# Modulation sums issued a step later, value products in batches of three, a ring of four and a fifth split-weight tile

## The chip, the core and the metric

One core of a Trainium2 chip runs the whole program. The metric is the device time of one execution in microseconds (us). Three executions of the kernel before took 1661.31, 1668.17 and 1668.65 us, with a median of 1668.17 us.

## What is computed

A trunk of two layers. Each layer normalises 512 latent and 256 context tokens of width 1024, shifts and scales them with rows that a small matrix-vector product makes of a conditioning vector (the "modulation"), projects them once, runs three kinds of attention (A: windowed, 8 heads; B: 2-D neighbourhood, 4 heads; C: latent, 4 heads), adds the output projection under a gate, and then a squared-ReLU MLP under a gate. In the last layer the context is only needed as keys and values.

```python
mod = split(silu(c) @ w_ada[l] + b_ada[l], 6)        # 6 rows of 1024, for latent and for context
h = modulate(rmsnorm(x, g1), mod[0], mod[1]) @ w_in[l]
x = x + mod[2] * (concat(out_a, out_b, out_c) @ w_out[l])
x = x + mod[5] * (relu(modulate(rmsnorm(x, g2), mod[3], mod[4]) @ w1) ** 2 @ w2)
```

## The kernel before

All data are float32. A projection with 32-bit precision is made of three matmuls on TensorE: weight and activation are each split into a rounded high part and a low part, and high·high, high·low and low·high are added up in PSUM. So every weight block that is loaded (`raw`, 128x1024) is first turned into two tiles: ScalarE casts the high part `wh` (L460) and VectorE subtracts to get the low part `wl` (L461). Both come from one set of tiles with the tag `w4`, four in all: two weight blocks at a time.

**Attention.** `att_unit` (L595) handles four rows of 128 queries. TensorE makes scores (L614), VectorE evacuates them with a running minimum (L618, L625), ScalarE takes the exponential (L630), VectorE, ScalarE or GpSimd normalises (L634 to L638). Then for every block of 128 keys, a "turn" transposes the four probability tiles on TensorE (L665) into PSUM (two tiles `pst`), and ScalarE or VectorE copies the 128x512 result to a slot of the ring `pT_ring` (L670), which has `NPT` = 6 slots. A "product" is the pair of value matmuls of one key block (L679). Turns and products go in batches of `PVB` = 6 key blocks: first all turns of a batch, from the last to the first, then all its products, so that the batch begins with a product that waits for the newest copy. A unit has 2, 4, 5 or 6 key blocks, so it is one batch. There are 40 units.

**Modulation.** The first rows come from matmuls at the start (`ada_quarter`, L249) and during layer 0 (`ada_row`, L207). The MLP gate of layer 0 and the six rows of layer 1 are made on the side during the MLP of layer 0 by the generator `ada_dve` (L269). A step of it loads a 128x512 piece of the weights (`araw`, L279), and VectorE multiplies it with a column of the conditioning vector and adds it to an accumulator `acc` (L283, L285); two accumulators for latent and context, or one where only the latent row is needed. Sixteen steps make a row. Then a matmul with a matrix of ones sums the accumulators over the partitions (L291, called the sum below), and a few small operations and transfers finish the row. `step(n)` in the MLP code (L1181) runs n steps after each weight chunk, 97 in all; what is left runs after the last MLP group of layer 0 (L1191). The sum of a row is issued in the same call that begins the next row. Accumulators, `araw` tiles and the ReLU results of the MLP share nine 128x512 tiles with the tag `re`.

**MLP.** `mlp1` computes 128 hidden features at a time over all tokens (24 or 48 matmuls for a weight block, L1099 to L1101), `mlp2` adds four such blocks to the output (L1133 to L1135), `resid` multiplies with the gate (L735) and adds to the stream (L736).

**Order.** A scheduler sets the order on each engine: it simulates the program with its own costs, takes what is ready by priority (products and sums have a high one) and gives out tiles of a tag as they come free. Each engine then runs its list strictly in order, so an instruction that waits holds everything behind it. `FENCE` (L76) makes a few weight loads of the start wait for the arrival of a given load of modulation weights.

Of the kernel before, what the change touches and what calls it, by code (L numbers as in the profile page):

```python
# [28 lines left out]
HUGE = 3e38  # L29
PS = {"d": 2, "s": 3, "t": 2, "v": 1, "a": 1}  # L30
STEPS = 2
PVB = 6
NPT = 6
ADAB = 2
STEP5 = 3
PREP1 = 1
# [3 lines left out]
XN = "VA"  # L40
RFAST = "GV"
PUT = "A"
CAPS = {"tm": 4, "rt": 4, "pr": 8, "r0": 16, "re": 9, "raw": 4, "w4": 4, "xn": 12,
        "h1": 16, "h2": 16, "pg": 18, "cr": 1, "ct": 8, "kr": 5, "vc": 2, "kc": 8,
        "up": 4, "u": 16, "wf": 16, "of": 8, "fg": 2, "ga": 4}
PAD = ("pr", "tm", "xn", "pg", "up")
# [2 lines left out]
for _tag, _names in (  # L49
    ("tm", "ce tf shuf qkraw maskB rpb junk upraw qr uphi"),  # L50
    ("rt", "rtmp brow ar"),
    ("pr", "prob"),
    ("r0", "raw0"),
    ("re", "relu acc araw arow"),
    ("raw", "raw"),
    ("w4", "wh wl"),
    ("xn", "xn"),
    ("h1", "hT1"),
    ("h2", "hT2"),
    ("pg", "qs kh kl vtok bias oth otl"),  # L60
    ("cr", "craw"),
    ("up", "uph upl"),
    ("ct", "cth ctl ropeC"),
    ("kr", "krf krh krl qrh qrl"),
    ("vc", "vc"),
    ("kc", "kc qc"),
    ("u", "uh ul of fg"),
    ("wf", "wfh wfl"),
    ("ga", "gate"),
):  # L70
    for _n in _names.split():
        TAGS[_n] = _tag
ADAPOS = [9, 18, 27]
FIN = ["vv", "vv", "gg", "gW"]
RLAST = "VV"
FENCE = {"pw0": 4, "pw1": 6, "w3": 24, "w4": 30, "rA": 31, "mA": 31}  # L76


@with_exitstack
def hybrid_dit_kernel(  # L80
# [30 lines left out]
    def prob(n, name="prob"):  # L111
        return sbuf(n, F32, name)

    def view(t_, shape):
        n = int(np.prod(shape))
        t_ = t_[:, :n]
        return t_ if len(shape) == 1 else t_.rearrange("p (a b) -> p a b", a=shape[0])
# [68 lines left out]
    V.tensor_scalar(nsink, sink, -1.0, None, ALU.mult)  # L186
    pT_ring = cp.tile([P, NPT, 512], F32, name="pT_ring")
    pT_n = [0]
# [80 lines left out]
    def ada_dve(l, ms):  # L269


        for m in ms:
            nw = 1 if l == DEPTH - 1 and m > 1 else 2
            acc = [[prob(512, name="acc") for _ in range(2)] for _ in range(nw)]
            for h in range(2):
                for k in range(KC):
                    raw = temp(512, name="araw")
                    c0 = m * D + h * 512
                    nc.sync.dma_start(raw, w_ada[l, k * P:(k + 1) * P, c0:c0 + 512])  # L279
                    for w in range(nw):  # L280
                        a_ = acc[w][h]
                        if k == 0:
                            V.tensor_scalar(a_, raw, ct[:, k, w:w + 1], None, ALU.mult)  # L283
                        else:
                            V.scalar_tensor_tensor(a_, raw, ct[:, k, w:w + 1], a_, ALU.mult, ALU.add)  # L285
                    yield

            ps = ps_d()
            with tc.high_priority():
                for j in reversed(range(2 * nw)):  # L290
                    T.matmul(ps[32 * j:32 * j + 32, :], ones, acc[j // 2][j % 2], start=True, stop=True,  # L291
                             tile_position=(0, 32 * j))
            rows = slice(0, 64 * nw)
            if m in (2, 5):
                gd = dp.tile([2, D], F32, name=f"gate{l}_{m}")
                br = prob(512, name="arow")
                for j in range(2 * nw):
                    c0 = m * D + (j % 2) * 512
                    nc.sync.dma_start(br[32 * j:32 * j + 32], b_ada[l:l + 1, c0:c0 + 512].partition_broadcast(32))
                V.tensor_tensor(br[rows], br[rows], ps[rows], ALU.add)  # L300
                for j in range(2 * nw):
                    nc.sync.dma_start(gd[j // 2:j // 2 + 1, (j % 2) * 512:(j % 2 + 1) * 512],
                                      br[32 * j:32 * j + 1])
                gdram[l, m] = gd
            else:
                mt = cp.tile([P, KC, 2], F32, name=f"mod{l}_{m}")
                ar = prob(512, name="arow")
                V.tensor_copy(ar[rows], ps[rows])
                pt = ps_d()
                for q in range(4):  # L310
                    T.transpose(pt[:, q * P:q * P + 64 * nw], ar[rows, q * P:(q + 1) * P], ident[rows, rows])
                p4 = pt.rearrange("p (q j c) -> p q j c", q=4, j=4)
                for w in range(nw):
                    V.tensor_tensor(mt[:, :, w].rearrange("p (h q) -> p q h", h=2), p4[:, :, 2 * w:2 * w + 2, 0],
                                    bT[:, l, m, :].rearrange("p (h q) -> p q h", h=2), ALU.add)
                modT[l, m] = mt
            ada_done.add((l, m))
# [277 lines left out]
    def att_unit(kind, rows, vap, put, sinkcols=None):  # L595
# [88 lines left out]

        for i in range(0, len(order), PVB):
            for item in reversed([turn(kb, i + j) for j, kb in reversed(list(enumerate(order[i:i + PVB])))]):
                product(*item)
# [51 lines left out]
    for l in range(DEPTH):  # L739
# [126 lines left out]
        if l == 0:  # L866
            rA = const([2, 512], ropeA, "ropeA")
# [446 lines left out]
```

## Time and profile before

| | |
|---|---|
| median of three executions | 1668.17 us (1661.31 to 1668.65) |
| the profiled execution | 1664.65 us |
| its span from first to last instruction | 1662.8 us |
| TensorE busy | 1596.6 us (96%) |
| TensorE weight loads busy (beside the matmuls) | 1364.9 us (82%) |
| VectorE busy | 1031.8 us (62%) |
| ScalarE busy | 689.4 us (41%) |
| GpSimd busy | 614.3 us (37%) |
| mean granted TensorE clock | 0.988 of full |

Instructions are named by their line of the kernel before (L291). An arrow `psd<-acc,ones` gives the output tile and the inputs; PE is TensorE, DVE VectorE, ACT ScalarE, POOL GpSimd, SP the queue that issues the transfers. The granted clock is a share of 2.4 GHz: 0.50 is 1.2 GHz. "Idle before" is the time an engine stood still ahead of an instruction, with what ended it.

### The profile page before, as it was taken

The numbers are of one execution on the slowest core, as the hardware profiler recorded it, in microseconds if no ns is written. First come the engines' busy times: TensorE is split into PE (matmuls) and PEld (weight loads), VectorE is DVE, ScalarE is ACT, GpSimd is POOL, SyncE is SP. The second block draws the span as 40 slices with busy tenths as digits, with TensorE's granted clock in tenths as the row PEclk, the third lists the DMA queues.
The fourth block names the chain that finished last, engine by engine and source line by source line (L and its number), as shares of the span: only waits on it lengthen the run. The fifth ranks groups of instructions, "written<-read, shape, count | busy, mean of one in ns | idle before, by whom it ended". The sixth has DMA issues, their size and how long they took to land.

```text
span 1662.8 us, 24084 instructions
## 1 busy us (share of the span) xinstructions
PE 1596.6 (96%) x8994; PEld 1364.9 (82%) x8994; DVE 1031.8 (62%) x1995; ACT 689.4 (41%) x1342; POOL 614.3 (37%) x564
## 2 busy tenths in 40 slices
PE   6999999999999999999999999999999899999997
PEld 3888789777898998988989789878776788888886
DVE  3565866787887576554455966776786644444446
ACT  5454467655631222312213154536765532332332
POOL 1111743643424253341523431143462333333335
PEclk8999999999999999999999999999999999999999
DMA  9653401120243333334333613211130133333331
GB/s 314 183 164 114 143 27 47 59 65 1 81 154 126 125 103 111 114 103 129 95 104 119 226 39 91 58 47 51 44 90 25 45 101 98 92 102 93 97 120 58
DMA packets 156421, 164.46 MB, mean 99 GB/s; under 512 B 8960, under 2 KB 111368, under 8 KB 156304
## 3 DMA queue, kind: packets, MB, share of 16 engines
q1 hardware_dynamic: 156304, 162.92, 32.2%
q8 instruction: 71, 1.16, 0.3%
q14 instruction: 46, 0.38, 0.1%
HBM read 155.53 MB, written 2.12 MB: 95 GB/s over the span
## 4 chain that ended last, share of the span: by engine, by line
PE 84%; DVE 7%; ACT 3%; DMA 2%; issue 2%; POOL 1%; SPq 1%; POOLq 0%; DVEq 0%; ACTq 0%
PE psd L1100 8%; PE psd L1099 8%; PE psd L1101 8%; PE psv L679 5%; PE pss L614 5%; PE pst L665 4%; PE pss L1133 3%; PE pss L1134 3%; PE pss L1135 3%; PE psd L477 3%; PE psd L479 3%; PE psd L478 3%; DVE wl L461 2%; PE psv L1133 1%; PE psa L1134 1%
## 5 line engine op out<-in xcount | busy, mean ns | idle before, releaser
L460 ACT CAST wh<-raw 128x1024 fp32r<-128x1024 f32 (+1 forms) x168 | 175.3, 1044 | 514.5 <-PE psd L1100 186.2
L461 DVE TENSOR_TENSOR wl<-raw,wh 128x1024 fp32r<-128x1024 f32 (+1 forms) x168 | 221.5, 1319 | 253.1 <-ACT wh L460 252.4
L736 POOL TENSOR_TENSOR xlat<-xlat,rtmp 128x512 f32<-128x512 f32 x159 | 236.9, 1516 | 263.6 <-DVE rtmp L735 261.9
L1099 PE MATMUL psd<-hT,wh 128*128 128x384 f32 (+2 forms) x752 | 265.8, 354 | 4.5 <-DVE hT L424 3.0
L1100 PE MATMUL psd<-hT,wl 128*128 128x384 f32 (+2 forms) x752 | 264.9, 352 | 3.7 <-DVE wl L461 3.7
L1101 PE MATMUL psd<-hT,wh 128*128 128x384 f32 (+2 forms) x752 | 265.3, 353 | 0.3 <-POOL hT L426 0.3
L638 POOL TENSOR_TENSOR prob<-prob,sm 128x512 f32<-128x512 f32 (+3 forms) x110 | 126.8, 1160 | 273.0 <-DVE sm L631 205.1
L1108 POOL TENSOR_TENSOR relu<-relu 128x384 f32<-128x384 f32 (+1 forms) x96 | 93.5, 976 | 332.5 <-ACT uh L1107 284.6
L630 ACT ACTIVATE prob<-prob,m 128x513 f32<-128x513 f32 (+6 forms) x160 | 120.9, 756 | 102.0 <-DVE m L625 58.7
L1099 PEld LDWEIGHTS psd<-hT,wh 128*128 128x128 f32 x752 | 141.7, 189 | 18.4 <-DVE hT L424 3.5
L1100 PEld LDWEIGHTS psd<-hT,wl 128*128 128x128 f32 x752 | 141.9, 189 | 14.3 <-DVE wl L461 4.6
L1101 PEld LDWEIGHTS psd<-hT,wh 128*128 128x128 f32 x752 | 141.7, 188 | 10.1 <-POOL hT L426 0.9
L285 DVE SCALAR_TENSOR_TENSOR acc<-araw,consts,acc 128x512 f32<-128x512 f32 x140 | 132.2, 968 | 6.3 <-DMA araw<-in_w_ada_dram 5.4
L1109 DVE TENSOR_TENSOR ul<-relu,uh 128x384 fp32r<-128x384 f32 (+1 forms) x96 | 60.7, 633 | 92.4 <-POOL relu L1108 92.3
L665 PE MATMUL pst<-consts,prob 128*128 128x128 f32 x688 | 106.6, 278 | 4.3 <-POOL prob L638 3.2
L665 PEld LDWEIGHTS pst<-consts,prob 128*128 128x128 f32 x688 | 80.6, 141 | 27.3 <-issue 11.2
L477 PE MATMUL psd<-hT,wh 128*128 128x384 f32 (+1 forms) x280 | 97.8, 349 | 2.3 <-ACT wh L460 1.3
L479 PE MATMUL psd<-hT,wl 128*128 128x384 f32 (+1 forms) x280 | 96.9, 347 | 1.1 <-DVE wl L461 1.1
L478 PE MATMUL psd<-hT,wh 128*128 128x384 f32 (+1 forms) x280 | 96.8, 346 | 0.0
L1134 PE MATMUL pss<-wl,uh 128*128 128x512 f32 x224 | 87.5, 390 | 0.0
L1135 PE MATMUL pss<-wh,ul 128*128 128x512 f32 x224 | 87.2, 390 | 0.0
L1106 ACT ACTIVATE relu<-psd 128x384 f32<-128x384 f32 (+1 forms) x93 | 48.6, 522 | 92.8 <-PE psd L1101 92.8
(265 smaller groups left out, 3550.8 us busy)
## 6 DMA issues: line engine op xcount, KB each, us to landing
raw<-in_w_mlp_in_dram SPq DMA_DIRECT2D x64, 512.0 KB, 4.3
raw<-in_w_mlp_out_dram SPq DMA_DIRECT2D x64, 512.0 KB, 4.4
araw<-in_w_ada_dram SPq DMA_DIRECT2D x112, 256.0 KB, 4.7
raw<-in_w_in_dram SPq DMA_DIRECT2D x24, 512.0 KB, 5.5
raw<-in_w_ada_dram SPq DMA_DIRECT2D x24, 512.0 KB, 4.3
raw<-in_w_ada_dram SPq DMA_DIRECT2D x32, 256.0 KB, 6.0
raw<-in_w_out_dram SPq DMA_DIRECT2D x8, 512.0 KB, 4.4
raw<-in_w_out_dram SPq DMA_DIRECT2D x16, 256.0 KB, 3.5
```

The source lines that it names most:

```text
L460: A.copy(hi, raw)
L461: V.tensor_tensor(lo, raw, bc(hi), ALU.subtract)
L477: T.matmul(ps[:, :n], wh[:, k, :], hh[k][:, s0:s0 + n], start=(k == 0), stop=False)
L478: T.matmul(ps[:, :n], wh[:, k, :], hl[k][:, s0:s0 + n], start=False, stop=False)
L479: T.matmul(ps[:, :n], wl[:, k, :], hh[k][:, s0:s0 + n], start=False, stop=(k == KC - 1))
L665: T.transpose(pt[:, r * P:(r + 1) * P], pts[r][:, pos[r][kb]:pos[r][kb] + P], ident)
L736: (V if fast and (RLAST if fast == "end" and t == 3 else RFAST)[dh] == "V" else G).tensor_tensor(xt[t][:, cs], xt[t][:, cs], tmp, ALU.add)
L1099: T.matmul(o_, wh[:, k, :], hh[k][:, sl], start=(k == 0), stop=False)
L1100: T.matmul(o_, wl[:, k, :], hh[k][:, sl], start=False, stop=False)
L1101: T.matmul(o_, wh[:, k, :], hl[k][:, sl], start=False, stop=(k == KC - 1))
L1134: T.matmul(a_, uh[:, ts_], wl[:, c % 2, :], start=False, stop=False)
L1135: T.matmul(a_, ul[:, ts_], wh[:, c % 2, :], start=False, stop=fin)
```

## The change

- `PVB` 6 to 3 and `NPT` 6 to 4: turns and products now go three key blocks at a time, and the ring has four slots. A unit of 4 to 6 key blocks becomes two batches.
- The four accumulators of a row become one 128x2048 tile with a tag of its own, `ac`, of which there is one. The tag `re` falls from nine tiles to five.
- `ada_dve` yields once more ahead of the sum. A row takes 17 steps in place of 16, and its sum comes a step after its last accumulation.
- The tag `w4` rises from four tiles to five. The memory in use stays the same: the ring gives up 4 KB per partition and `w4` takes them; `re` gives up 8 KB and `ac` takes them.
- The fence of the weight load of columns 1152 on waits for load 5 of the modulation weights in place of load 30.

```diff
-PVB = 6
-NPT = 6
+PVB = 3
+NPT = 4
-CAPS = {"tm": 4, "rt": 4, "pr": 8, "r0": 16, "re": 9, "raw": 4, "w4": 4, "xn": 12,
+CAPS = {"tm": 4, "rt": 4, "pr": 8, "r0": 16, "re": 5, "ac": 1, "raw": 4, "w4": 5, "xn": 12,
-    ("re", "relu acc araw arow"),
+    ("re", "relu araw arow"),
+    ("ac", "acc"),
-FENCE = {"pw0": 4, "pw1": 6, "w3": 24, "w4": 30, "rA": 31, "mA": 31}
+FENCE = {"pw0": 4, "pw1": 6, "w3": 24, "w4": 5, "rA": 31, "mA": 31}
@@ ada_dve
-            acc = [[prob(512, name="acc") for _ in range(2)] for _ in range(nw)]
+            acc = view(prob(2048, name="acc"), [4, 512])
+            acc = [[acc[:, 2 * w + h_] for h_ in range(2)] for w in range(nw)]
             for h in range(2):
                 for k in range(KC):
...
                     yield
+            yield
 
             ps = ps_d()
             with tc.high_priority():
                 for j in reversed(range(2 * nw)):
                     T.matmul(ps[32 * j:32 * j + 32, :], ones, acc[j // 2][j % 2], start=True, stop=True,
```

In the changed kernel lines are numbered three higher from the sum on (L294 is the sum, L461 becomes L464, L679 becomes L682). The orders below are those of the built programs. Three places are shown.

**First place: the sum of the third row of layer 1 (its attention gate), during the MLP of layer 0.** TensorE before; `wh_7604` and `wl_7605` are one weight block of `mlp1`, `wl_7691` is the next:

```order
L1100 MATMUL psd_7611<-hT2_4864,wl_7605 128x384
L1101 MATMUL psd_7611<-hT2_4872,wh_7604 128x384
L291 MATMUL psd_7673<-acc_7000,ones_83 32x512
L291 MATMUL psd_7673<-acc_6999,ones_83 32x512
L1099 MATMUL psd_7696<-hT2_4857,wh_7690 128x384
L1100 MATMUL psd_7696<-hT2_4857,wl_7691 128x384
```

VectorE before, up to the last accumulation of that row (`acc_7000`); `wl_7765` is the low part of the block after the next:

```order
L461 TENSOR_TENSOR wl_7605<-raw_7602,wh_7604 128x1024
L1109 TENSOR_TENSOR ul_7535<-relu_7586,uh_7534 128x384
L461 TENSOR_TENSOR wl_7691<-raw_7688,wh_7690 128x1024
L285 SCALAR_TENSOR_TENSOR acc_7000<-araw_7596,consts_66,acc_7000 128x512
L285 SCALAR_TENSOR_TENSOR acc_7000<-araw_7599,consts_66,acc_7000 128x512
L1109 TENSOR_TENSOR ul_7535<-relu_7591,uh_7534 128x384
L1109 TENSOR_TENSOR ul_7609<-relu_7660,uh_7608 128x384
L461 TENSOR_TENSOR wl_7765<-raw_7762,wh_7764 128x1024
L285 SCALAR_TENSOR_TENSOR acc_7000<-araw_7670,consts_66,acc_7000 128x512
```

TensorE after the change, the same sum (`acc_7126`); the weight block in use is `wh_7733` and `wl_7734`, the next is `wh_7821` and `wl_7822`:

```order
L1102 MATMUL psd_7740<-hT2_4864,wh_7733 128x384
L1103 MATMUL psd_7740<-hT2_4864,wl_7734 128x384
L294 MATMUL psd_7799<-acc_7126,ones_83 32x512 x2
L1104 MATMUL psd_7740<-hT2_4872,wh_7733 128x384
L1136 MATMUL pss_7813<-wh_7821,uh_6977 128x512
```

VectorE after the change:

```order
L464 TENSOR_TENSOR wl_7734<-raw_7731,wh_7733 128x1024
L287 SCALAR_TENSOR_TENSOR acc_7126<-araw_7651,consts_66,acc_7126 128x512
L287 SCALAR_TENSOR_TENSOR acc_7126<-araw_7654,consts_66,acc_7126 128x512
L1112 TENSOR_TENSOR ul_7590<-relu_7646,uh_7589 128x384
L1112 TENSOR_TENSOR ul_7664<-relu_7715,uh_7663 128x384
L464 TENSOR_TENSOR wl_7822<-raw_7819,wh_7821 128x1024
L287 SCALAR_TENSOR_TENSOR acc_7126<-araw_7725,consts_66,acc_7126 128x512
L287 SCALAR_TENSOR_TENSOR acc_7126<-araw_7728,consts_66,acc_7126 128x512
L1112 TENSOR_TENSOR ul_7664<-relu_7720,uh_7663 128x384
L1112 TENSOR_TENSOR ul_7738<-relu_7789,uh_7737 128x384
L464 TENSOR_TENSOR wl_7864<-raw_7861,wh_7863 128x1024
```

Before, two low parts stood on VectorE between the block in use at the sum and the row's last accumulation; now one stands there.

**Second place: the third unit of attention C in layer 1, TensorE.** Before, up to its products:

```order
L614 MATMUL pss<-kc,qc 128x256 x3
L665 MATMUL pst<-consts,prob 128x128 x8
L614 MATMUL pss<-kc,qc 128x512 x3
L665 MATMUL pst<-consts,prob 128x128 x10
L679 MATMUL psv<-pT_ring,vc 64x256 x12
L665 MATMUL pst<-consts,prob 128x128 x6
L717 MATMUL psd<-wh,oth 128x512
```

After the change:

```order
L668 MATMUL pst<-consts,prob 128x128 x8
L617 MATMUL pss<-kc,qc 128x256 x3
L617 MATMUL pss<-kc,qc 128x512 x3
L682 MATMUL psv<-pT_ring,vc 64x256 x6
L668 MATMUL pst<-consts,prob 128x128 x10
L682 MATMUL psv<-pT_ring,vc 64x256 x6
L668 MATMUL pst<-consts,prob 128x128 x6
L720 MATMUL psd<-wh,oth 128x512
```

The twelve products, which followed directly on the transpositions, are now two groups of six: the first behind six score matmuls, the second directly behind ten transpositions, of which the last two belong to the next unit.

**Third place: the end of the output projection and the first MLP matmuls in layer 1, TensorE.** Before:

```order
L717 MATMUL psd_12891<-wh_12817,oth_12569 128x512
L718 MATMUL psd_12891<-wl_12818,oth_12569 128x512
L719 MATMUL psd_12891<-wh_12817,otl_12570 128x512
L1099 MATMUL psd_13071<-hT2_12935,wh_13065 128x256
L416 MATMUL pst_12993<-consts_66,xn_12903 128x128
L416 MATMUL pst_12993<-consts_66,xn_12907 128x128
L1100 MATMUL psd_13071<-hT2_12935,wl_13066 128x256
```

After the change:

```order
L720 MATMUL psd_12878<-wh_12804,oth_12556 128x512
L721 MATMUL psd_12878<-wl_12805,oth_12556 128x512
L722 MATMUL psd_12878<-wh_12804,otl_12557 128x512
L419 MATMUL pst_12959<-consts_66,xn_12889 128x128
L419 MATMUL pst_12959<-consts_66,xn_12893 128x128
L1102 MATMUL psd_13058<-hT2_12922,wh_13052 128x256
L1103 MATMUL psd_13058<-hT2_12922,wl_13053 128x256
```

The order of these matmuls is nearly the same. On ScalarE the cast of the first high part, `wh_13065` before, stood behind all exponentials of attention C of this layer; now, as `wh_13052`, it stands ahead of them all.

## Rows read from the trace of the kernel before

**Rows 1.** Page, part 1: busy time, share of the span, instructions.

```profile
PE 1596.6 (96%) x8994; PEld 1364.9 (82%) x8994; DVE 1031.8 (62%) x1995; ACT 689.4 (41%) x1342; POOL 614.3 (37%) x564
```

**Rows 2.** Windows: stretch, its length, busy time per engine, granted clock, DMA.

```profile
0.00:40.00 40.00, 24.23 (x242) 13.86 (x243) 14.93 (x40) 20.05 (x44) 4.96 (x9) 0.83 1.01 314
40.00:440.00 400.00, 388.06 (x2595) 329.22 (x2594) 279.00 (x752) 227.71 (x516) 156.25 (x172) 0.99 0.30 88
440.00:960.00 520.00, 513.50 (x2614) 460.18 (x2613) 325.24 (x406) 133.65 (x210) 189.45 (x153) 1.00 0.39 124
960.00:1300.00 340.00, 319.68 (x1963) 269.63 (x1962) 243.00 (x602) 193.11 (x415) 129.07 (x127) 0.99 0.20 57
1300.00:1640.00 340.00, 337.93 (x1531) 281.38 (x1531) 153.57 (x177) 107.44 (x142) 124.45 (x95) 1.00 0.30 90
```

**Rows 3.** TensorE's waits: line, releaser: total us, times, longest.

```profile
PE psa L258 <- DMA raw<-in_w_ada_dram: 14.3, 7, 9.5
PE psv L679 <- ACT pT_ring L670: 5.2, 7, 1.8
PE psd L291 <- DVE acc L285: 4.5, 2, 3.5
PE psd L1100 <- DVE wl L461: 3.7, 3, 2.3
PE pst L665 <- ACT pT_ring L670: 0.9, 2, 0.6
PE psv L679 <- DVE pT_ring L670: 0.8, 1, 0.8
```

**Rows 4.** Timeline, TensorE's two waiting sums: start, us, instruction, idle before.

```profile
756.44 1.92 PE L291 MATMUL psd<-acc,ones 128*32 128x512 f32 x4 [3.54 <-DVE acc L285]
954.43 1.05 PE L291 MATMUL psd<-acc,ones 128*32 128x512 f32 x4 [0.92 <-DVE acc L285]
```

**Rows 5.** Timeline of VectorE just ahead of the first of these sums.

```profile
753.84 1.23 DVE L461 TENSOR_TENSOR wl<-raw,wh 128x1024 fp32r<-128x1024 f32 x1 [2.52 <-ACT wh L460]
754.98 1.32 DVE L285 SCALAR_TENSOR_TENSOR acc<-araw,consts,acc 128x512 f32<-128x512 f32 x1
```

**Rows 6.** Windows of 2 us behind two idle times of TensorE.

```profile
1300.00:1302.00 2.00, 2.00 (x10) 1.85 (x10) 1.97 (x6) 0.56 (x1) 0.34 (x1) 0.50 0.58 176
...
757.00:759.00 2.00, 2.00 (x6) 0.71 (x3) 0.76 (x2) 0.00 (x0) 0.00 (x0) 0.50 0.56 205
759.00:761.00 2.00, 2.00 (x10) 2.00 (x10) 0.08 (x1) 0.00 (x0) 0.00 (x0) 0.80 0.17 15
```

**Rows 7.** Timeline of TensorE in the second layer's attention.

```profile
1048.20 2.17 PE L679 MATMUL psv<-pT_ring,vtok 128*64 128x256 f32 x20 [1.81 <-ACT pT_ring L670]
...
1275.04 2.81 PE L679 MATMUL psv<-pT_ring,vc 128*64 128x256 f32 x24 [0.97 <-ACT pT_ring L670]
1277.78 0.88 PE L665 MATMUL pst<-consts,prob 128*128 128x128 f32 x6
1278.41 0.48 PE L717 MATMUL psd<-wh,oth 128*128 128x512 f32 x1
1278.73 0.39 PE L718 MATMUL psd<-wl,oth 128*128 128x512 f32 x1
1278.96 0.40 PE L717 MATMUL psd<-wh,oth 128*128 128x512 f32 x1
```

**Rows 8.** Timeline of TensorE, first MLP matmuls of the second layer.

```profile
1294.88 0.39 PE L1099 MATMUL psd<-hT,wh 128*128 128x256 f32 x1 [0.41 <-ACT wh L460]
...
1297.82 0.39 PE L1100 MATMUL psd<-hT,wl 128*128 128x256 f32 x1 [2.33 <-DVE wl L461]
```

**Rows 9.** Page, part 6: modulation weight loads, KB, us to landing.

```profile
araw<-in_w_ada_dram SPq DMA_DIRECT2D x112, 256.0 KB, 4.7
```

**Rows 10.** Page, part 5: accumulations and weight casts.

```profile
L285 DVE SCALAR_TENSOR_TENSOR acc<-araw,consts,acc 128x512 f32<-128x512 f32 x140 | 132.2, 968 | 6.3 <-DMA araw<-in_w_ada_dram 5.4
L460 ACT CAST wh<-raw 128x1024 fp32r<-128x1024 f32 (+1 forms) x168 | 175.3, 1044 | 514.5 <-PE psd L1100 186.2
```

## The prediction

> **What bounds the kernel now.** I read the page first: TensorE is busy 1596.6 us of a span of 1662.8 us, no other engine is above two thirds [rows 1]. The change removes no matmul, so at most the 66 us in which TensorE stands idle can be won, plus what it loses by running slower behind an idle time. The windows by stage say where they lie [rows 2]: 40.00 - 24.23 = 15.8 us in the first 40 us, 400.00 - 388.06 = 11.9 in layer 0's attention, 520.00 - 513.50 = 6.5 in its MLP, 340.00 - 319.68 = 20.3 from 960 to 1300 us (change of layer and attention of layer 1), 2.1 in most of the last MLP; the rest is the tail. The reader is to see that the MLP stages have nearly no idle time, and that attention and the change of layer have two thirds of what is not start or end. Then TensorE's waits by releaser [rows 3]: the largest, 14.3 us, is for loads at the start, where the transfers run at a share of 1.01 [rows 2]. Of what the change touches there are three kinds: value products or transpositions that wait for a copy to the ring (5.2 + 0.9 + 0.8 = 6.9 us, ten times), the sums (4.5 us, two times) and low weight parts (3.7 us, three times).
>
> **The sums.** The wait of 3.54 us [rows 4] is a ring of dependences that the first place of the order shows. The sum stands on TensorE behind the last matmul of the weight block in use. On VectorE its last accumulation stands behind the low part of the block after the next. With four tiles for split weights that block can only be cast when the block in use has been given back, which is at the sum's door: VectorE begins that low part at 753.84 us, after an idle time that ended with the cast, and the accumulation at 754.98 us [rows 5]; the sum starts at 756.44. After the change only the next block's low part stands between, and the fifth tile lets its cast go ahead. I went through all seven sums in both orders: before, this is the only one with two low parts between in the MLP, and after, none has. So 3.5 us go. Behind this idle time TensorE ran at 0.50 of its clock for 2 us and at 0.80 for the next 2 [rows 6], that is at 1.2 GHz in place of 2.4 for part of them: 0.5 x 2 + 0.2 x 2 = 1.4 us more. I take -4.9 us. Bounds: 0, if the delay shows up at another matmul; -5.8, if the other sum's 0.92 us [rows 4] goes as well.
>
> **Batches of three.** Ring waits cost 6.9 us now; the longest are 1.81 and 0.97 us [rows 7], where products follow their newest transposition directly. To price a gap in the order: six transpositions take 1278.41 - 1277.78 = 0.63 us (0.105 each), 24 records of products 1277.78 - 1275.04 = 2.74 us (0.114 each), a matmul of 512 columns 1278.96 - 1278.73 = 0.23 [rows 7]. The 40 batches become 72. By these prices two of the 72 have 0.2 us of other work or less between newest transposition and first product, four have 0.74 to 0.80, all others over 1 us; before, five had 0.2 us or less. I take 0.97 us for the two and half of it for the four, 3.9 us, so -3.0 us. Bounds: -6.9, if all are hidden, and +4.7, if all twelve with under 1.4 us between wait 0.97 us (11.6 - 6.9). The four slots cost nothing by themselves: one turn of the next batch still fits beside a batch of three, where six slots took a batch of six and no more.
>
> **More changes of kind.** The first matmul of the output projection after transpositions takes 1278.73 - 1278.41 = 0.32 us where the next takes 0.23 [rows 7]: 0.09 us for a change of kind. Products now stand next to split matmuls at 68 places in the order, at 37 before. 31 x 0.09 = +2.8 us. No row prices a product behind such a matmul alone, so the bounds are 0 and twice that, +5.6.
>
> **The fifth tile for split weights.** ScalarE waits 514.5 us in all ahead of weight casts, most of it for TensorE to give tiles back [rows 10], but TensorE has 2.1 us of idle time in 340 us of the last MLP [rows 2], so a cast that comes sooner is worth nothing there. It is worth something where an MLP begins: at 1294.88 and 1297.82 us TensorE waits 0.41 us for the first high part and 2.33 us for its low part [rows 8]. The third place shows the same order of matmuls, but the cast, 1.04 us [rows 10], now stands ahead of attention C. What stays is the low part behind the release of a tile: I take -1.5 us (the 0.41 and a cast). Bounds: 0, as VectorE is the one that is late there, and -3.7, the 2.74 us and the 0.5 x 2 us lost at 1300 us [rows 6].
>
> **Seventeen steps in place of sixteen.** Of 97 steps in layer 0's MLP 7 x 17 = 119 are now needed, 112 before; 22 in place of 15 are left for the end, 20 of them with an accumulation: five more, 5 x 0.968 = 4.8 us of VectorE [rows 10], and five loads, moved into the change of layer. On SP they stand between the loads of layer 1's first projection weights as before; each takes 4.7 us to land [rows 9], and with five tiles in flight that is one per 0.94 us, just the pace of an accumulation. The transfers of bias and gate that follow a sum move with it; the gates are not due before layer 1's output projection. The last sum now has 99 matmul rows behind the first use of the last MLP weight block, 76 before: 23 x 0.23 = 5.3 us more room, which pays for the 4.8. I take +1 us for TensorE. Bounds: 0 and +6.2 (4.8 and a clock loss of 1.4). The single accumulator tile makes a new row wait for the sum of the last; VectorE stands behind that sum anyway, as it reads its result ahead of the new row. I cost it at nothing; if the sum is late, that wait is the same one.
>
> **The fence.** The order on SP up to this load is the same but for one exchange. 512 KB at the 314 GB/s of that stretch [rows 2] are 1.7 us: 0, between -1.7 and +1.7.
>
> **Sum.** -4.9 - 3.0 + 2.8 - 1.5 + 1.0 + 0 = -5.6 us. The profiled execution took 1664.65 us, 3.5 below the median of the three and 3.3 above the lowest; 1664.65 - 5.6 = 1659.1, and as the median lies higher I forecast 1660 us. About 0.5% (8.3 us) is what a measurement of this kernel can tell from no change; -5.6 us is 0.34%.
>
> **Rivals.**
> - *More goes.* The scheduler fills attention so well that sums, ring waits and the start of the MLP all reach their lower bounds: -5.8 - 6.9 + 2.8 - 3.7 = -13.6, some 1651 us. For it: layer 1's attention holds most of the 20.3 us [rows 2], and short batches leave something else to do between. Against it: waits on normalisation and scores are untouched.
> - *The wait moves into the change of layer.* The last sum waits for the five accumulations, and the MLP's start gains nothing: -4.9 - 3.0 + 2.8 + 6.2 = +1.1, 1665.8 us. For it: that sum waits 0.92 us already [rows 4]. In this case the fifth tile and the later step do not do what they say.
> - *Slower: short batches wait for their own copies.* Twice as many batches have a newest copy, and each may wait 0.97 us [rows 7]. With a third of the 72 waiting, 24 x 0.97 = 23.3 us in place of 6.9, the sum is -4.9 + 16.4 + 2.8 - 1.5 + 1.0 = +13.8, 1678.5 us. It decides for slower from 19 such waits on (18.4 - 6.9 - 2.6 = 8.9 us). Against it: the order has twelve batches with less than 1.4 us between.
> - *Slower: short batches lower the clock.* If each of the 32 added batches lost the 1 us that the stretch from 757 us shows at half clock [rows 6], 32 us would come on top of the sum: 1691 us. Against it: the granted clock is 0.99 over both attention stages [rows 2], which change kind all the time, and 0.50 behind idle time. The Trainium skill has a rule for this side: its page Perfetto Trace Analysis, section Matmul Optimizations, says that the matmul engine scales its power with use, so that matmuls should run back to back in batches. The trace agrees as to idle time and does not as to the size of batches.
>
> **How the numbers follow.** Forecast 0.45, more goes 0.22, the wait moves 0.20, copies 0.08, clock 0.02; 0.03 for what I do not see. The forecast's case lies across the line of 0.5%, with its smaller half beyond it: 0.22 + 0.20 = 0.42 for faster. The last two rivals make 0.10 for slower. Within 0.5%: 0.48. The range goes from 1650, just past the case in which more goes, to 1671, which takes in the moved wait and 5 us of its bounds and of the runs' scatter; the slower rivals stay outside.
>
> **What would show it.** Right: no sum in the middle of layer 0's MLP waits over 1 us for an accumulation, and the clock stays at 1.00 around it; TensorE's waits on ring copies sum to 3 to 5 us, most of them in attention C; the first low part of layer 1's MLP costs under 1.5 us; idle time from 440 to 960 us falls to some 3 us; TensorE's busy time rises by 1 to 3 us less what the clock gives back. Wrong: more than 15 waits on ring copies; a sum or a hidden part at the change of layer that waits 3 us or more; new idle time in the MLP; a first 40 us that differ by more than 2 us.

## Result, and the profile after

The changed kernel takes 1644.15 us (median; 1643.35 to 1647.55), the kernel before, beside it, 1667.77 us: a ratio of 0.9877 with a 95% interval of [0.9862, 0.9892]. By that ratio it takes some 20.5 us less; the two medians differ by 23.6. The forecast of 1660 us (1650 to 1671) lies 16 us too high, and the time is outside its range. The profiled execution of the changed kernel took 1647.55 us with a span of 1645.8, against 1664.65 and 1662.8 before. Its mean granted clock is 0.995, against 0.988.

Part 1 of its page answers to [rows 1], the windows after them to [rows 2]:

```profile
PE 1594.6 (97%) x8994; PEld 1361.1 (83%) x8994; DVE 1009.0 (61%) x1995; ACT 682.6 (41%) x1342; POOL 608.3 (37%) x564
```

```profile
0.00:40.00 40.00, 23.24 (x234) 13.08 (x235) 14.28 (x39) 19.99 (x43) 4.58 (x9) 0.96 1.01 318
40.00:440.00 400.00, 391.42 (x2601) 328.89 (x2601) 278.45 (x752) 228.74 (x518) 151.26 (x173) 1.00 0.30 88
440.00:960.00 520.00, 515.69 (x2634) 463.48 (x2633) 314.44 (x407) 131.33 (x212) 194.69 (x154) 1.00 0.40 124
960.00:1300.00 340.00, 326.88 (x2044) 276.64 (x2042) 251.30 (x623) 199.47 (x426) 129.09 (x132) 0.99 0.22 61
```

The span is 17.0 us shorter: TensorE's busy time fell by 2.0 us and its idle time by 15.0, from 66.2 to 1645.8 - 1594.6 = 51.2. The windows show where: 16.8 us idle at the start (15.8 before), 8.6 in layer 0's attention (11.9), 4.3 in its MLP (6.5), 13.1 from 960 to 1300 us (20.3). TensorE's waits on sums, on split weights and on the ring, as in [rows 3]:

```profile
PE psd L294 <- DVE acc L287: 2.6, 1, 2.6
PE psd L1103 <- DVE wl L464: 2.3, 3, 0.8
PE pss L1103 <- DVE wl L464: 1.4, 1, 1.4
PE psd L482 <- DVE wl L464: 1.1, 2, 0.8
PE psv L682 <- DVE pT_ring L673: 1.1, 2, 0.6
PE pss L499 <- DVE wl L464: 0.8, 1, 0.8
PE pst L668 <- ACT pT_ring L673: 0.3, 1, 0.3
```

Ring waits fell from 6.9 to 1.4 us. Of the sums only the last waits, 2.6 us. And no wait on a cast of a high part is left. Before, there were such waits, in the same view, and I had not counted them:

```profile
PE psd L1099 <- ACT wh L460: 1.5, 3, 0.7
PE psd L477 <- ACT wh L460: 1.3, 2, 0.7
PE psd L479 <- DVE wl L461: 1.1, 3, 0.5
PE pss L1133 <- ACT wh L460: 1.0, 1, 1.0
PE psd L718 <- DVE wl L461: 0.8, 1, 0.8
PE pss L496 <- DVE wl L461: 0.3, 1, 0.3
```

With the 3.7 us of [rows 3] TensorE waited 9.7 us for split weights before, and waits 5.6 now. 3.8 of the 9.7 us were for high parts.

### The profile page after: what moved, and what is told of

It is laid out like the page before. It is cut to its first block, busy times and chain, and to the rows that moved or that the text cites. A ratio compares the mean times of both kernels' runs of the same rounds, so it can differ in the third digit from the quotient of the medians.

```text
span 1645.8 us, 24134 instructions
## 1 busy us (share of the span) xinstructions
PE 1594.6 (97%) x8994; PEld 1361.1 (83%) x8994; DVE 1009.0 (61%) x1995; ACT 682.6 (41%) x1342; POOL 608.3 (37%) x564
## 4 chain that ended last, share of the span: by engine, by line
PE 85%; DVE 7%; DMA 4%; issue 2%; ACT 2%; POOL 0%; SPq 0%; POOLq 0%; DVEq 0%; ACTq 0%
PE psd L1102 8%; PE psd L1103 8%; PE psd L1104 8%; PE pss L617 5%; PE psv L682 5%; PE pst L668 4%; PE psd L480 3%; PE psd L482 3%; PE psd L481 3%; PE pss L1138 3%; PE pss L1136 3%; PE pss L1137 3%; PE psd L720 2%; PE psd L722 2%; PE psd L721 2%
## 5 line engine op out<-in xcount | busy, mean ns | idle before, releaser
L464 DVE TENSOR_TENSOR wl<-raw,wh 128x1024 fp32r<-128x1024 f32 (+1 forms) x168 | 219.0, 1304 | 184.1 <-issue 82.0
L1109 ACT ACTIVATE relu<-psd 128x384 f32<-128x384 f32 (+1 forms) x93 | 49.1, 528 | 280.5 <-PE psd L1104 278.1
L287 DVE SCALAR_TENSOR_TENSOR acc<-araw,consts,acc 128x512 f32<-128x512 f32 x140 | 117.7, 867 | 6.6 <-DMA araw<-in_w_ada_dram 5.8
```

Source lines behind the costliest of these rows:

```text
L464: V.tensor_tensor(lo, raw, bc(hi), ALU.subtract)
```

## Experiments

Each kernel was timed in five rounds beside the kernel before. The table gives the ratio to it and, from TensorE's timeline of the one profiled execution, the length of five stages in us. A0: from the start to the first MLP matmul of layer 0; S0: on to the first output matmul; M0: on to layer 1's first transposition; A1: on to layer 1's first MLP matmul; S1: on to its first output matmul. From there to TensorE's last matmul it takes 304.8 us in all of them but two (305.2 in three + two, 310.2 in six tiles), and 8.4 to 10.0 us more to the last instruction (9.6 before, 8.4 after). Names like 3 + 2 give the tiles for high parts and for low parts; "four keys" is explained below.

Three pairs of these kernels show how far one profile can be trusted. In the traces changed and "five in one ring, four keys" run the same instructions in the same order on TensorE, VectorE, ScalarE and GpSimd, and so do three + two and "3 + 2, four keys", and 2 + 2 and 2 + 3 with four keys. Their ratios differ by 0.0001 to 0.0012, but the length of a stage by up to 3.5 us (S0 72.6 and 69.1).

| kernel | median us | ratio [95%] | A0 | S0 | M0 | A1 | S1 |
|---|---|---|---|---|---|---|---|
| before | 1667.8 | 1 | 425.0 | 67.3 | 487.1 | 315.5 | 53.5 |
| changed | 1644.2 | 0.9877 [0.9862, 0.9892] | 425.4 | 65.1 | 484.5 | 305.0 | 52.5 |
| batches alone | 1660.2 | 0.9972 [0.9960, 0.9985] | 429.3 | 67.5 | 487.0 | 307.4 | 52.8 |
| sums alone | 1661.0 | 0.9979 [0.9969, 0.9989] | 427.0 | 67.9 | 481.9 | 314.9 | 53.5 |
| all but the fifth tile | 1655.7 | 0.9943 [0.9928, 0.9958] | 430.6 | 67.7 | 481.7 | 308.2 | 53.3 |
| all but the later step | 1645.1 | 0.9880 [0.9867, 0.9894] | 423.9 | 65.3 | 482.6 | 303.9 | 52.6 |
| ring of six, four tiles | 1666.3 | 1.0005 [0.9995, 1.0016] | 431.1 | 68.5 | 481.8 | 313.5 | 55.0 |
| batches of two | 1660.0 | 0.9973 [0.9964, 0.9982] | 427.5 | 65.0 | 482.0 | 319.1 | 50.2 |
| six tiles, three raw | 1654.3 | 0.9943 [0.9931, 0.9955] | 429.5 | 59.9 | 485.1 | 315.6 | 47.0 |
| seven probabilities | 1650.5 | 0.9918 [0.9900, 0.9936] | 425.1 | 65.0 | 482.9 | 310.0 | 51.9 |
| 3 + 2, seven probabilities | 1657.1 | 0.9953 [0.9941, 0.9965] | 427.0 | 65.9 | 482.2 | 313.7 | 52.9 |
| 2 + 3, seven probabilities | 1672.8 | 1.0049 [1.0032, 1.0066] | 433.4 | 72.4 | 485.7 | 315.0 | 53.5 |
| three + two | 1645.9 | 0.9881 [0.9867, 0.9894] | 425.1 | 64.1 | 482.1 | 306.3 | 52.0 |
| 2 + 2, four keys | 1663.5 | 0.9991 [0.9980, 1.0003] | 426.3 | 72.6 | 483.5 | 308.2 | 56.1 |
| 2 + 3, four keys | 1663.4 | 0.9990 [0.9980, 1.0000] | 428.5 | 69.1 | 483.9 | 309.7 | 56.0 |
| 3 + 2, four keys | 1646.8 | 0.9893 [0.9879, 0.9907] | 424.5 | 65.6 | 483.0 | 307.6 | 52.0 |
| five in one ring, four keys | 1642.8 | 0.9872 [0.9858, 0.9886] | 423.7 | 65.3 | 482.4 | 302.4 | 52.5 |

### The parts alone

**Batches alone** (the kernel before with two edits):

```diff
-PVB = 6
-NPT = 6
+PVB = 3
+NPT = 4
```

> Batches of three and a ring of four alone. Theory 'batches' (the part of the gain that I missed comes from TensorE having other work at the ends of short batches, mostly in the attention of layer 1): at least 8 us faster than before, ratio 0.995 or less, ring waits of TensorE under 3 us in place of 6.9, and the sum wait of 3.5 us in the MLP of layer 0 still there. Theory 'fifth tile' (weight parts that come sooner clear the attention stages): within 4 us of before, as the four tiles stay. Theory 'any new order' (the order before happens to be a bad one): faster by 5 us or more, but no more so than the other single parts.

**Sums alone** (`acc` as one tile, `re` 9 to 5, the later step; all else as before):

> One accumulator tile, five tiles in place of nine for the rest, and the sum a step later; batches of six, ring of six and four weight tiles as before. My term for the sum: 3 to 6 us faster, ratio 0.9965 to 0.998, the wait of 3.5 us and the half clock behind it gone. 'Batches' and 'fifth tile' expect no more than that and no change in the attention of layer 1. 'Any new order' expects 8 us or more with a different layer 1 attention.

**All but the fifth tile** (the changed kernel):

```diff
-"w4": 5
+"w4": 4
```

> The changed kernel with four weight tiles in place of five. 'Batches': like the changed kernel within 5 us, ratio to before 0.987 to 0.991; only the start of layer 1's MLP gives back some 1.5 us. 'Fifth tile': gives back 8 us or more, ratio 0.993 or above. 'Any new order': anything between.

**The fence alone** (the kernel before with `"w4": 5` in place of 30 in `FENCE`):

> The fence of one weight load alone; the order of TensorE, ScalarE and GpSimd stays word for word. All theories: within 2 us of before, ratio 0.999 to 1.001, first 40 us alike. If the start of the program differs by more than 1 us, the fence has a part in the change.

The fence gave a ratio of 1.0004 [0.9993, 1.0015]: nothing. Its one profile has 18.1 us of idle time in the first 40 us, 2.3 more than the kernel before and more than the 1 us that was expected; the ratio shows none of it. By their ratios batches and sums alone took 4.7 and 3.5 us off, together 8.2, and all but the fifth tile 9.5 us: these two add up. The rest, 0.9943 - 0.9877 of 1668 us, some 11 us, comes with the fifth tile, which the sum of the prediction had at 1.5. The theory 'batches' missed twice: it had asked for 8 us from batches alone, and for all but the fifth tile within 5 us of the changed kernel. By stage the fifth tile took 5.2 us off A0, 2.6 off S0, 3.2 off A1 and 0.8 off S1, and M0 became 2.8 longer.

### Which fifth tile

In the run with four tiles ScalarE waits long for tiles, with the cast at the head of its queue; in the changed kernel that row is gone. Of ScalarE's longest waits, the first and the fourth with four tiles, and after them the first with the five of the change:

```profile
ACT wh L463 <- PE psd L1103: 192.2, 60, 5.1
...
ACT relu L1109 <- PE psd L1104: 90.2, 32, 11.6
```

```profile
ACT relu L1109 <- PE psd L1104: 278.1, 89, 11.3
```

The wait has only changed its place, from the cast to the activation behind it: 192.2 + 90.2 = 282.4 us before, 278.1 after. From this I made two theories, 'the queue' and 'depth', and gave the tiles out by name, which takes the same memory for three high and two low as for five in one ring. For two high and three low another tile has to make room in memory, so both kernels had a tile of probabilities less. Diff of the first; the second has `"wh": 2, "wl": 3`:

```diff
-    ("w4", "wh wl"),
+    ("wh", "wh"),
+    ("wl", "wl"),
-"pr": 8
-"w4": 5
+"pr": 7
+"wh": 3, "wl": 2
```

> The changed kernel with the five tiles for split weights given out by name: three for high parts, two for low parts; the pool of probabilities has seven tiles instead of eight, because the packing needs the room (the next kernel has it too). Theory 'the queue': with four tiles the cast of a high part stands at the head of ScalarE's queue until TensorE lets go of a tile (192.2 us in 60 waits for the MLP's first products and 24.5 us in 10 for the projections, in the run with four tiles; none of either in the changed kernel), and what is queued behind it on ScalarE comes later. Three tiles for high parts keep the head of the queue free, so the whole gain stays: ratio to the kernel before 0.990 or less (the changed kernel: 0.988), and no wait of the cast for those products. Theory 'depth': what counts is that half a weight more may be prepared, whichever half: 0.990 or less here too. Theory 'any new order': between 0.988 and 0.996.

> The same with two tiles for high parts and three for low parts, again seven tiles of probabilities. Theory 'the queue': the casts on ScalarE wait for TensorE again as with four tiles (some 190 us in the trace), so the fifth tile's gain is lost: ratio to the kernel before 0.993 or more (with four tiles in all it was 0.994), some 10 us above the kernel with three and two. Theory 'depth': 0.990 or less, within 4 us of the kernel with three and two. Theory 'any new order': between 0.988 and 0.996, and the difference between the two kernels has nothing to do with the casts' waits.

**Six tiles** in one ring, with `"raw"` 4 to 3:

> The changed kernel with six tiles for split weights and three tiles instead of four for the raw weights. Theory 'the queue': five tiles have freed ScalarE of its wait already, so a sixth brings nothing; three raw tiles hold transfers back. 1644 to 1652 us, ratio 0.986 to 0.991. Theory 'depth': half a weight more again, another few us less: ratio below 0.985. Should the loads have become the limit, it is slower than that: TensorE then waits for casts that wait for DMAs, ratio above 0.991.

**All but the later step** (the `yield` ahead of the sum taken out again):

> The changed kernel without the step between the last multiplication of the modulation rows and their sum over partitions; all else as changed. If it is this delay that takes away the two waits for the rows in the middle of the MLP (4.5 us in the trace before), they come back and the time is 3 to 5 us above the changed kernel: ratio 0.990 to 0.992, and two waits of TensorE for the rows of over 0.5 us inside the MLP of layer 0. If the accumulator in one tile and the new order do it without the step: within 1.5 us of the changed kernel.

Three and two is 15.7 us shorter than two and three, but it kept only a part of the gain, and what it lost lay nearly all in A1 (313.7 us, the changed kernel 305.0). Six tiles fell back to 0.9943 with the longest A1 but one: a theory of tiles alone does not tell this. Its S0 and S1 are the shortest, but what S1 lost (5.5 us against the changed kernel) the rest gained (5.4): the first output matmul only stands earlier. Nor were the loads the limit, as its expectation feared: TensorE waited 2.4 us for split weights, the least of all these kernels. The later step is worth nothing that can be measured: 0.9880 without, 0.9877 with it. The two waits of the kernel before did not come back; the only one on a sum is the last, 0.4 us. Next came the trim by itself, and the sizes of batch and ring:

**Three + two** with eight tiles of probabilities, and **seven probabilities** with the five tiles in one ring (`"pr"` 8 to 7 alone):

> Three tiles for high parts and two for low parts as before, now with all eight tiles of probabilities. In the run with seven, the start, the attention of layer 0 and the MLP of layer 0 were as long as in the changed kernel (925.8 us to the output products against 923.2), and all of the loss lay in the attention of layer 1 (293.8 us against 285.2). If the lost tile of probabilities did that: the attention of layer 1 takes 284 to 287 us again, ratio to the kernel before 0.987 to 0.991. If the fixed names of the tiles did it: 293 us again, ratio 0.994 to 0.997. If the list scheduler's order is a draw in that stage: anything between, 0.987 to 0.997.

> The changed kernel with seven tiles of probabilities instead of eight, the five tiles for split weights in one ring. If the lost tile of probabilities is what made the two kernels by name longer: the attention of layer 1 goes from 285.2 to some 294 us and the ratio to the kernel before is 0.992 to 0.996. If it was the split by name: ratio 0.986 to 0.990 as the changed kernel.

**Batches of two** (`PVB = 2` in the changed kernel), and **ring of six, four tiles** (`NPT = 6`, `"w4": 4`):

> The changed kernel with value products issued by twos instead of threes, the ring still of four tiles. If smaller batches gain because a ring tile comes free sooner: the waits of the first product for its tile and of the transposition for a ring tile fall further, 1640 to 1644 us, ratio 0.983 to 0.987. If the changes between transpositions and products begin to cost (the half as many batches again, at the 0.09 us for each that the sum took): slower than the changed kernel by 2 to 5 us, ratio 0.989 to 0.992. If the order of the list scheduler is what moved: no sign to be told, 0.983 to 0.996.

> The kernel with four tiles for split weights (batches of three, ring of four, sums in one tile; ratio 0.9943) with the ring of six again. If the ring of four is what lengthened the attention of layer 0 (370.5 us against 366.2 before), this run is back at 366 us there and keeps the shorter attention of layer 1 (286 us against 293.6): ratio 0.990 to 0.993. If the batches of three did both, the ring's size changes nothing: 0.993 to 0.996.

Three and two with eight tiles has the whole gain, 0.9881. The lost tile of probabilities costs 0.004 by itself, and more together with names. Batches of two lose 16 us against three, and the ring of six loses 11 against the ring of four; both came out slower than any of their theories had it. Most of the first (14.1 us) and half of the second (5.3) lie in A1, whose length goes from 302.4 to 319.1 us over the table. Waits on the ring do not explain that: they are 4.8 us with batches of two against 1.4 in the changed kernel, and 2.7 with the ring of six against 3.1 with the ring of four. Nor did A0 become shorter with the ring of six, as its expectation asked (431.1 us, 430.6 with four slots). The scheduler wrote attention anew at each of these edits, so one pair of kernels cannot price one tile. The last four kernels therefore share one trim (`"kr"` 5 to 4, which left the orders of the changed kernel and of three + two as they were) and their code differs in the split tiles alone:

> The changed kernel with the tiles for split weights given out by name, two for high parts and two for low parts, and with four tiles of rotated keys instead of five, for the packing (the next three too): the base of these four. Theory 'third high part': as with four tiles in one ring, 0.993 to 0.999 of the kernel before; the starts of the MLPs as long as before (67 and 53 us). Theory 'draw' (each order of the list scheduler lands anywhere within 1%): nothing to be told of the four but that they scatter.

> Two for high parts, three for low parts, four tiles of rotated keys. Theory 'third high part': within 0.004 of the kernel with two and two, since the third low tile waits for a high part all the same; the starts of the MLPs stay at 67 and 53 us or more. Theory 'any fifth tile': 5 to 12 us below the kernel with two and two. Theory 'draw': anywhere.

> Three for high parts, two for low parts, four tiles of rotated keys. Theory 'third high part': 5 to 15 us below both kernels with two high parts; the start of layer 0's MLP at 64 to 66 us. Theory 'any fifth tile': as the kernel with two and three. Theory 'draw': not below both of the others by more than 4 us.

> The five tiles in one ring, as changed, with four tiles of rotated keys: the high part of a weight takes the tile of the low part three weights before, the low part that of the high part two weights before. Theory 'third high part': within 0.002 of the kernel with three and two by name. Theory 'draw': may differ from it by up to 0.01.

Two and two takes 1663.5 us, with starts of the MLPs (72.6 and 56.1 us) longer than the 67 and 53 that were expected, and two and three 1663.4: a third low tile is worth nothing, and it changes no order. Three and two takes 1646.8: **the third tile for high parts is worth 16.7 us** here. The order changed with it (about a third of TensorE's 8994 records stand elsewhere), so this price includes what the scheduler made of the tile. But with seven probabilities it was 15.7 us the same way, and in the ring 11. The one ring of five, in which a high part takes the tile of a low part of three weights before, has it too (1642.8). 'Depth' falls, and so does 'the queue' as I had it. The cast's long wait for the MLP's first products is absent with two and two, which is slow, and it is back with six tiles (198.1 us). ScalarE's wait for the MLP's products is nearly as long in both; the waits of two and two, then of three and two:

```profile
ACT relu L1110 <- PE psd L1105: 296.7, 92, 12.1
```

```profile
ACT relu L1110 <- PE psd L1105: 281.0, 91, 11.3
```

What differs is at what moment the next high part is there. TensorE's waits for split weights, all of them, with two and two:

```profile
PE psd L1103 <- ACT wh L464: 4.0, 3, 1.7
PE psd L481 <- ACT wh L464: 3.3, 2, 1.9
PE psd L1104 <- DVE wl L465: 3.0, 3, 1.6
PE pss L1137 <- ACT wh L464: 1.5, 1, 1.5
PE psd L483 <- DVE wl L465: 1.0, 3, 0.4
PE pss L500 <- DVE wl L465: 0.3, 1, 0.3
```

and with three and two:

```profile
PE psd L1104 <- DVE wl L465: 2.1, 3, 0.8
PE pss L1104 <- DVE wl L465: 1.6, 1, 1.6
PE psd L483 <- DVE wl L465: 0.4, 1, 0.4
PE pss L500 <- DVE wl L465: 0.3, 1, 0.3
```

That is 13.1 us against 4.4, and with two and three the rows are those of two and two but for 0.1 us. Of the six waits on high parts with two and two, four (6.6 of 8.8 us) lie where two weight blocks have been in use side by side and a third follows: at 59.65, 451.79, 1005.64 and 1311.21 us. The other two stand at the first output block of layer 0's MLP and at the first block of layer 1's. All kernels with two high tiles or a ring of four wait for a high part at these six places: 8.8 or 8.9 us in all with two high tiles by name, 3.8 to 4.1 with the ring of four. With three high tiles, or a ring of five or six, no such wait is left but a single one of 1.5 us without the later step. The rows of all but the fifth tile, in the ring of four:

```profile
PE psd L1102 <- ACT wh L463: 1.8, 3, 0.7
PE psd L480 <- ACT wh L463: 1.3, 2, 0.7
PE pss L1136 <- ACT wh L463: 1.0, 1, 1.0
```

One of the four, the third block of layer 0's MLP, TensorE and then ScalarE, with two and two:

```profile
449.56 0.34 PE L1105 MATMUL psd<-hT,wh 128*128 128x384 f32 x1
449.74 0.34 PE L1105 MATMUL pss<-hT,wh 128*128 128x384 f32 x1
451.79 0.62 PE L1103 MATMUL psd<-hT,wh 128*128 128x384 f32 x2 [1.71 <-ACT wh L464]
453.05 0.69 PE L1104 MATMUL psd<-hT,wl 128*128 128x384 f32 x1 [0.64 <-DVE wl L465]
```

```profile
449.93 0.49 ACT L1110 ACTIVATE relu<-psd 128x384 f32<-128x384 f32 x1 [2.41 <-PE psd L1105]
450.32 0.48 ACT L1110 ACTIVATE relu<-pss 128x384 f32<-128x384 f32 x1
450.69 1.05 ACT L464 CAST wh<-raw 128x1024 fp32r<-128x1024 f32 x1
```

The two blocks (outputs `psd` and `pss`) end side by side, at 449.90 and 450.08 us, and read both high tiles until then; behind two activations the cast takes from 450.69 to 451.74, and TensorE starts at 451.79. In the ring of four of the kernel before, the same place costs 0.44 us; TensorE and then ScalarE:

```profile
447.07 0.33 PE L1100 MATMUL psd<-hT,wl 128*128 128x384 f32 x1
447.59 0.33 PE L1101 MATMUL psd<-hT,wh 128*128 128x384 f32 x1
448.55 0.62 PE L1099 MATMUL psd<-hT,wh 128*128 128x384 f32 x2 [0.44 <-ACT wh L460]
```

```profile
447.45 1.05 ACT L460 CAST wh<-raw 128x1024 fp32r<-128x1024 f32 x1 [1.89 <-PE psd L1100]
448.40 0.48 ACT L1106 ACTIVATE relu<-psd 128x384 f32<-128x384 f32 x1
```

Here the cast starts as soon as the last matmul with a low part has ended (447.40), while a high part is still to be read at 447.59: in the ring the new high part can take a low part's tile, and the cast stands ahead of the activations. With three and two, TensorE at the same place:

```profile
447.86 0.34 PE L1105 MATMUL pss<-hT,wh 128*128 128x384 f32 x1
448.04 0.34 PE L1103 MATMUL psd<-hT,wh 128*128 128x384 f32 x1
448.82 0.45 PE L1104 MATMUL psd<-hT,wl 128*128 128x384 f32 x1 [0.45 <-DVE wl L465]
```

The high part is there, and TensorE goes on without a gap until the low part, 0.45 us. The clock can add to the price. The windows behind the two places, two and two first:

```profile
452.00:460.00 8.00, 7.36 (x26) 7.04 (x26) 8.00 (x10) 2.31 (x5) 3.91 (x3) 0.57 0.71 219
```

```profile
449.00:457.00 8.00, 8.00 (x47) 8.00 (x48) 7.10 (x8) 4.46 (x8) 4.42 (x4) 1.00 0.77 235
```

At a granted clock of 0.57 (1.2 GHz most of the time in place of 2.4) 26 matmul records fall into 8 us, against 47. How much of the 16.7 us this makes is not shown: two and three, with the order of two and two, has no such fall here and the same median. Over all their executions (12, 11 and 4) the mean granted clock is 0.988 with two and two, 0.989 with two and three and 0.993 with three and two.

## Why the prediction was wrong, by its steps

- **The fifth tile: the step that failed.** The prediction said that a cast that comes sooner is worth nothing but where an MLP begins, and took -1.5 us with a bound of -3.7. It argued from the last MLP's long stretch of one weight block after another, which still holds (304.8 us in nearly all kernels), and priced the start of layer 1's MLP alone. The waits on high parts of 1.5 + 1.3 + 1.0 us stood in the same view as [rows 3], and I left them out. Shown in its place: 11 us between the kernels with and without the fifth tile, and 16.7 us for a third high tile against two by name, where nothing else in the code differs. With a ring of four TensorE waits for a high part at six places, 4.1 us in all, of which the prediction priced one, 0.41 us. In the profiles of two and two and of three and two 8.7 us are waits (13.1 - 4.4), and the stages S0 and S1, where an MLP starts, hold 7.0 + 4.1 us, part of that the clock. Two and two has more to gain than the ring of four, as its casts of high parts come later (1.71 us of wait against 0.44 at the place above). Of the ring's 11 us the waits are only a part: all waits for split weights together fall from 8.1 to 5.6 us with the fifth tile, while the two profiled spans differ by 10.0 us and A0 and A1, where the order of attention changed, became 8.4 us shorter. What in that order saves the time was not found.
- **Batches of three.** -3.0 for ring waits and +2.8 for changes of kind, -0.2 together; alone they gave -4.7 us. Alone they left 3.4 us of ring waits, near the 3.9 of the sum; in the changed kernel, with the fifth tile beside them, 1.4 are left, nearer to the bound of -6.9. The term for changes of kind was real and a little larger. The value products of `vtok` with sums alone, and with batches alone:

```profile
L682 PE MATMUL psv<-pT_ring,vtok 128*64 128x256 f32 (+1 forms) x496 | 59.2, 379 | 4.3 <-ACT pT_ring L673 3.5 <-DVE pT_ring L673 0.8
```

```profile
L679 PE MATMUL psv<-pT_ring,vtok 128*64 128x256 f32 (+1 forms) x496 | 62.9, 383 | 2.4 <-ACT pT_ring L670 1.4 <-DVE pT_ring L670 0.9
```

  That is +3.7 us in this group. But A0 became 4.3 us longer and A1 8.1 shorter with them, by the whole new order of attention. By the timeline A1's waits of over 0.15 us fell from 17.0 to 9.6 us, and only 3.0 us of this are ring waits. The sum had no term for the rest. With a ring of six (and four split tiles) A1 is back at 313.5 us, so it is not the batches' size alone that gives it; what in the order does was not found.
- **The sums.** -4.9 was right in place and near in size: M0 is 5.2 us shorter with sums alone, the whole kernel 3.5, and no sum waits in the middle of an MLP. The mechanism named was half wrong: the waits are gone with the later step and no fifth tile (sums alone), and with the fifth tile and no later step. A kernel with the one accumulator tile and neither of the two was not run.
- **Change of layer.** +1, up to 6.2: the last sum waited 2.60 us in the profile after, 0.39 without the later step, but also 0.50 in "five in one ring, four keys", which runs the order of the changed kernel. The medians do not differ by it.
- **Fence.** 0, as measured.
- **The clock.** The rival of a slower clock fell: it is 0.995 with 32 more batches. Summed over windows of 4 us between 48 and 1636 us, the time at the lower clock is 20.4 us before and 10.3 after, 27.4 with two and two, 17.1 with two and three and 17.2 with three and two; so one order can differ by 10 us from one execution to the next. The clock fell behind idle time, though not behind all of it (last section), and the added batches did not lower it. The rule of the Trainium skill (Perfetto Trace Analysis, section Matmul Optimizations), that matmuls should run back to back in batches because the engine scales its power with use, goes with these traces as to idle time and not as to the size of batches.
- **Which case it was.** 'More goes', at 1651 us with a chance of 0.22, came nearest, still 7 us too high: its bound for the fifth tile was -3.7. It looked to layer 1's attention, where most of the gain lies (A1 10.5 of the 17.0 us), but put the gain there down to ring waits. These give 4.6 of it, so its time came near partly by luck. The signs named for the forecast came as said for the first low part of layer 1's MLP (0.80 us). Ring waits of 3 to 5 us (1.4), idle time of 3 us from 440 to 960 (4.3) and a busy time 1 to 3 us higher (2.0 lower) did not come.

## What to carry to other kernels

Where an engine that is 97% busy reads weights that other engines prepare, look at the places where the pattern changes, not at the steady stretch: a pair of blocks that ends together gives back its tiles at nearly the same time, and then one tile more for the part that is needed first can be worth more than its wait shows (16.7 us against 8.7 here). Count every wait on one kind of resource before a term is called small. And where a scheduler may rewrite the order at each edit, compare several pairs that differ in one thing, and look whether their orders differ: here one unrelated tile (of probabilities) moved the time by 6 us, and another (of rotated keys) left the order as it was both times it was taken away alone.

## What was not expected of the hardware

Two kernels with the same order and the same waits did not get the same clock in their profiles. Two and three waits at the same place (1.72 us, and 0.64 behind it) and its windows show no fall there, where two and two fell to 0.57; S0 is 69.1 us against 72.6, while the medians are 1663.4 and 1663.5 us. The rows of two and three:

```profile
452.00:456.00 4.00, 2.08 (x10) 1.75 (x11) 2.73 (x4) 3.81 (x7) 0.94 (x2) 1.00 0.05 12
456.00:460.00 4.00, 4.00 (x25) 4.00 (x24) 4.00 (x5) 0.49 (x1) 2.97 (x2) 1.00 0.95 288
```

So a price for the clock, like the 1.4 us that the prediction took from [rows 6], holds for an execution here, not for a wait.
